# A two-layer hybrid decoder on one core: an opening that streams two matrices, an end in three token parts, and new priorities

## The chip, the core and the metric

The kernel runs on one core of a Trainium2 chip. A core has five engines with an instruction stream each: TensorE (PE, matmuls into PSUM, with its weight loads as PEld), VectorE (DVE), ScalarE (ACT), GpSimd (POOL) and SyncE (SP), which here issues most of the DMAs. The metric is device time of one execution in microseconds, as the median of several runs. A profile is one more execution, with every instruction's start and length.

## The reference, cut to what matters

512 tokens of width 1024 go through two layers. In each layer one normalised input is projected to the channels of three groups of heads:

```python
def hybrid_layer(x, ...):
    h = rms_norm(x, norm1_g)
    (qa, ka, va, qi, ki, wi, qb, kb, vb, rb, gl, uc) = split_cols(h @ w_in)
    qa, ka, qi, ki = (partial_rope(y, cos, sin) for y in (qa, ka, qi, ki))
    o_a = dsa_attention(qa, ka, va, qi, ki, wi)   # top 128 keys by the indexer's score
    o_b = gla_chunked(qb, kb, vb, log_a)          # gated linear attention
    o_b = rms_norm(o_b, gla_norm_g) * silu(rb)
    o_c = multiscale_pool(uc, w_pool, pool_scale)
    x = x + concat(o_a, o_b, o_c) @ w_out
    return x + conv_glu_ffn(rms_norm(x, norm2_g), w_up, conv_w, conv_b, w_down)
```

The indexer's score is the sum over 4 heads of wi * relu(qi . ki), and the top 128 keys of each token are kept. A final rms_norm follows the second layer. Everything is float32.

## The kernel before, in words

**Products.** The width of 1024 is 8 chunks of 128 channels, each a tile of 128 partitions x 512 tokens. To keep float32 accuracy each operand is split into a high part and the rest, and each product (`mm3`) is three matmuls: high x high, high x rest, rest x high. An activation chunk x gives xh (ACT) and xl (DVE), a piece of weights `raw` gives `hi` (ACT) and `lo` (DVE). Pieces of weights go through rings of tiles: 3 of `raw`, 5 each of `hi` and `lo` (`weights`, line 533). PSUM has four tiles for the large products (`mm`) and four for the small ones (`aux`).

**Normalisation.** The projections use x times the gain only; the factor for each token is applied when a product leaves PSUM ("evacuated"). `squares` sums the squares of the 8 chunks, `rstd` gets the token sums by matmuls with a column of ones, then the scale (DVE), the power (POOL, tile rt), and a broadcast over partitions by matmul (aux<-consts,rt). In the opening, 7 adds make the sum: 6 on POOL, the last on DVE.

**A layer** (`layer`, line 1091): the indexer's query (part "qi"), the token-major projection of vb, wi, ki and gl ("tok", 340 columns), keys and scores ("score1" to "score3"), the choice of the top keys by rounds of maxima on DVE ("top1" to "top3"), then rb (the gate of GLA) and gqk (query and key of GLA), GLA itself, v, the pooling branch, q and k, attention over 4 head pairs x 4 token blocks, and the output product. Tiles that have to change partitions or get rotated go through DMAs: sl to sa and sb, s0l and s1l, rot, sh. Then the feed-forward part in two halves of 11 chunks. 

**The end** (`finish`, line 1218): of the last down product the chunks 0 to 5 are done for all tokens; the last two (LATE) are done in two halves of 256 tokens, and after each half its statistics, its scaled outputs and its stores follow. A store holds 2 chunks of 256 tokens.

**The order.** The program's operations are first recorded with what each reads and writes (`Plan`). A list scheduler then simulates all engines with a price for each operation, forwards and backwards a few times; where several operations are ready, the priority decides, which is a distance to the end plus HASTE of the operation's part (a table, in ns). Rings and PSUM tiles are counted, so an operation can be held until a tile is free. Each engine then runs its list in order. All recorded operations are issued by one line, L488, so the profile is read by the names of tiles.

Of the kernel before, what the change touches and what calls it, by code (L numbers as in the profile page):

```python
# [493 lines left out]
class Kern:  # L494
# [594 lines left out]


    def layer(self, l):
# [34 lines left out]
        nc.part = "gqk"  # L1126
        w = self.weights(a["w_gqk"][l], KC, 256)
        ps = self.chunk(w, 0)
        gq = self.slot("gq")
        nc.vector.scalar_tensor_tensor(out=gq, in0=ps, scalar=32.0 ** -0.5, in1=self.rb, op0=OP.mult, op1=OP.mult)  # L1130
        ps = self.chunk(w, 1)
        gk = self.slot("gk")
        nc.vector.tensor_tensor(out=gk, in0=ps, in1=self.rb, op=OP.mult)
# [84 lines left out]
    def finish(self, gs):  # L1218
# [17 lines left out]
        for u in range(2):  # L1236
            blocks = (range(CUT), range(CUT, NB))[u]
            n0 = len(blocks) * P
            r = slice(blocks[0] * P, blocks[0] * P + n0)
# [22 lines left out]
    def run(self):  # L1262
# [20 lines left out]
        load(self.x[0], a["x"][:, 0, :])  # L1283
        self.w_first = self.weights(a["w_qi"][0][:, 0:256], 1, 256, whole=True)
        load(self.x[1], a["x"][:, 1, :])
        self.w_first += self.weights(a["w_qi"][0][:, 256:512], 1, 256, whole=True)
        load(self.vec[:, KC:], a["vec"][:, KC:])
        pos = self.small("pos", T // 16, I32)
        load(pos, a["pos"])
        for c in range(2, KC):  # L1290
# [100 lines left out]
```

## Time and profile before

| | |
|---|---|
| median of 3 runs | 1242.99 us (1242.94 to 1245.13) |
| profiled execution | 1244.28 us, span 1242.2 us |
| mean granted clock of TensorE | 0.990 of full speed |
| PE busy | 1213.9 us, 6160 matmul records |
| DVE busy | 702.3 us |
| ACT busy | 508.8 us |
| POOL busy | 333.4 us |

A row of the timeline gives the start, the length, the engine and the operation, as out<-in with shape and type, and in brackets the idle time ahead of it with what ended it. Records of a small matmul in float32 count twice, since it takes two passes. Matmuls overlap, so their pace is read from the starts.

### The profile page before, as it was taken

How to read it: one execution, taken by the hardware profiler on the slowest of the kernel's cores; microseconds unless marked ns; L12 is line 12 of the kernel's file. 1: busy time of each engine (PE TensorE's matmuls, PEld its weight loads, DVE VectorE, ACT ScalarE, POOL GpSimd, SP SyncE). 2: the span in 40 equal slices, each digit the busy share in tenths (PEclk: the TensorE clock that was granted, in tenths of full speed). 3: DMA queues.
4: the chain of work that ended last, by engine and by line, in shares of the span. 5: the costliest groups of instructions: out<-in, count | busy, mean ns of one | idle time of the engine just before them, and what ended most of it. 6: DMA issues, size and time to landing. Idle time of an engine off the chain costs nothing.

```text
span 1242.2 us, 16552 instructions
## 1 busy us (share of the span) xinstructions
PE 1213.9 (98%) x6160; PEld 998.0 (80%) x6160; DVE 702.3 (57%) x1244; ACT 508.8 (41%) x818; POOL 333.4 (27%) x284
## 2 busy tenths in 40 slices
PE   7999999999999999999999999999999999999996
PEld 5877778888888888888897777788888888888886
DVE  6479987445554344453455999645445534444433
ACT  5464247633332233333344533684334322333330
POOL 4164243222222022221206522512122300222111
PEclk9999989999999999999999999999999999999998
DMA  6422356123223332323543036533122333322321
GB/s 231 127 82 85 113 159 170 35 85 102 85 75 106 109 111 76 102 81 110 159 129 111 18 106 172 142 107 99 66 91 85 88 93 126 101 94 89 101 74 68
DMA packets 49392, 129.38 MB, mean 104 GB/s; under 512 B 7440, under 2 KB 10016, under 8 KB 49312
## 3 DMA queue, kind: packets, MB, share of 16 engines
q1 hardware_dynamic: 49200, 128.04, 33.5%
q8 instruction: 49, 0.80, 0.3%
q0 software_dynamic: 112, 0.28, 0.1%
q14 instruction: 31, 0.25, 0.1%
HBM read 109.22 MB, written 4.26 MB: 91 GB/s over the span
## 4 chain that ended last, share of the span: by engine, by line
PE 89%; DVE 3%; DMA 3%; POOL 2%; issue 1%; ACT 1%; SPq 1%; DVEq 0%; POOLq 0%; ACTq 0%
PE mm L488 80%; PE aux L488 9%; DVE lo L488 1%; DMA s0l<-sl 1%; DMA s1l<-sl 1%; SPq L488 1%; POOL qb L488 1%; DVE score L488 0%; DMA raw<-in_w_out 0%; DMA x<-in_x 0%; DVE m L488 0%; DMA q<-rot 0%; POOL sl L488 0%; DVE out L488 0%; ACT xh L488 0%
## 5 line engine op out<-in xcount | busy, mean ns | idle before, releaser
L488 PE MATMUL mm<-xh,hi 128*128 128x512 f32 x992 | 391.2, 394 | 2.9 <-ACT hi L488 1.2
L488 PE MATMUL mm<-xl,hi 128*128 128x512 f32 x992 | 387.5, 391 | 5.0 <-DVE xl L488 5.0
L488 PE MATMUL mm<-xh,lo 128*128 128x512 f32 x992 | 387.3, 390 | 0.0
L488 DVE TENSOR_TENSOR lo<-raw,hi 128x1024 fp32r<-128x1024 f32 (+5 forms) x217 | 263.7, 1225 | 180.5 <-ACT hi L488 178.6
L488 ACT ACTIVATE hi<-raw 128x1024 fp32r<-128x1024 f32 (+5 forms) x217 | 207.8, 965 | 339.3 <-PE mm L488 302.2
L488 PEld LDWEIGHTS mm<-xh,hi 128*128 128x128 f32 x992 | 186.8, 188 | 47.9 <-issue 4.9
L488 PEld LDWEIGHTS mm<-xl,hi 128*128 128x128 f32 x992 | 186.7, 188 | 44.0 <-DVE xl L488 7.1
L488 PEld LDWEIGHTS mm<-xh,lo 128*128 128x128 f32 x992 | 186.6, 188 | 39.4
L488 PE MATMUL mm<-h,hi 128*128 128x512 f32 (+1 forms) x470 | 180.0, 383 | 0.0
L488 PE MATMUL mm<-h,lo 128*128 128x512 f32 (+1 forms) x470 | 178.3, 379 | 0.0
L488 PE MATMUL mm<-l,hi 128*128 128x512 f32 (+1 forms) x470 | 178.3, 379 | 0.0
L488 POOL TENSOR_TENSOR cv<-cv,rstd 128x512 f32<-128x512 f32 x44 | 58.3, 1327 | 311.1 <-ACT cv L488 303.1
L488 POOL TENSOR_TENSOR l<-cv,h 128x512 fp32r<-128x512 f32 x44 | 70.5, 1601 | 150.3 <-ACT h L488 144.2
L488 PEld LDWEIGHTS mm<-h,lo 128*128 128x128 f32 x470 | 88.4, 188 | 16.7
L488 PEld LDWEIGHTS mm<-h,hi 128*128 128x128 f32 x470 | 88.5, 188 | 16.4 <-issue 0.5
L488 PEld LDWEIGHTS mm<-l,hi 128*128 128x128 f32 x470 | 88.5, 188 | 15.7
L488 ACT ACTIVATE cv<-a,vec 128x512 f32<-128x512 f32 x44 | 35.9, 815 | 144.3 <-DVE a L488 144.3
L488 DVE TENSOR_TENSOR a<-mm,rstd 128x512 f32<-128x512 f32 x44 | 30.4, 692 | 113.7 <-PE mm L488 113.7
L488 DVE SCALAR_TENSOR_TENSOR cv<-a,vec,cv 128x511 f32<-128x511 f32 x88 | 70.2, 799 | 34.2 <-ACT cv L488 32.8
L488 POOL TENSOR_TENSOR sq<-sq,sq 128x512 f32<-128x512 f32 x29 | 44.0, 1516 | 144.5 <-ACT sq L488 144.0
L488 DVE TENSOR_TENSOR x<-x,mm 128x512 f32<-128x512 f32 (+1 forms) x50 | 33.1, 665 | 83.3 <-PE mm L488 83.3
L488 DVE MATCH_REPLACE8 score<-m,score 128x512 f32<-128x512 f32 (+2 forms) x96 | 52.0, 545 | 0.0
(191 smaller groups left out, 1296.6 us busy)
## 6 DMA issues: line engine op xcount, KB each, us to landing
raw<-in_w_up SPq DMA_DIRECT2D x88, 512.0 KB, 3.9
raw<-in_w_down SPq DMA_DIRECT2D x32, 384.0 KB, 3.1
raw<-in_w_down SPq DMA_DIRECT2D x32, 320.0 KB, 2.9
raw<-in_w_qk SPq DMA_DIRECT2D x16, 512.0 KB, 3.9
raw<-in_w_out SPq DMA_DIRECT2D x16, 512.0 KB, 4.4
x<-in_x SPq DMA_DIRECT2D x16, 256.0 KB, 5.7
raw<-in_w_v SPq DMA_DIRECT2D x8, 512.0 KB, 4.2
raw<-in_w_rb SPq DMA_DIRECT2D x4, 512.0 KB, 4.2
```

Source lines behind the costliest of these rows:

```text
L488: self.issued(i, fn(*args, **kw))
```

## The change

1. Opening: every chunk of x is loaded, split and used at once with the two matrices qi and gqk, which come as pieces of two chunks x 256 columns into slots of their own (tiles first, fh and fl). Four PSUM tiles accumulate side by side, two for qi and two for gqk. The evacuation of gqk moves to a function `gated`. In the second layer both stay in their old places in the code.
2. All sums of squares of the opening are on DVE.
3. The end has three token parts, of 256, 128 and 128 tokens. The squares of the last two chunks aren't added to the sum by DVE: the matmuls with ones accumulate the sum and both chunks' squares in PSUM. A store of the narrow parts holds 4 chunks of 128 tokens.
4. The warm-up has 14 small matmuls instead of 8, rope tables get a part name, and HASTE gets new values. Two lines of that table are shown.

```diff
-HASTE = {"evac": 1200, "raw": -2700, "end0": -300, "top2": -48500, "gqk": -6300, "end": -118400, "gla": 900,
...
+         "rb": -6000, "tok": 900, "sq": -100, "gqk": 300, "rope": -17400, "ffn": -100, "end": 27900,
...
-WARM = 8
+WARM = 14
 LATE = 2
-CUT = 2
+ENDS = ((0, 1), (2,), (3,))
...
-            (nc.vector if m == KC - 1 else nc.gpsimd).tensor_tensor(out=self.ssum, in0=self.ssum, in1=sq, op=OP.add)
+            (nc.vector if m == KC - 1 or first else nc.gpsimd).tensor_tensor(out=self.ssum, in0=self.ssum, in1=sq, op=OP.add)
...
-    def rstd(self, blocks):
+    def rstd(self, blocks, more=()):
...
+        sums = (self.ssum, *more)
+        for i, x in enumerate(sums):
+            with nc.together():
+                for tb in blocks:
+                    nc.tensor.matmul(ps[:, tb:tb + 1], lhsT=x[:, tb * P:(tb + 1) * P], rhs=self.c("ones")[:, 0:1],
+                                     start=i == 0 and tb == at, stop=i == len(sums) - 1 and tb == blocks[-1])
+        return self.inverse(ps[:, at:at + n], blocks)
...
+    def gated(self, ps):
+
+        nc = self.pl
+        nc.part = "gqk"
+        gq = self.slot("gq")
+        nc.vector.scalar_tensor_tensor(out=gq, in0=ps[0], scalar=32.0 ** -0.5, in1=self.rb, op0=OP.mult, op1=OP.mult)
+        gk = self.slot("gk")
+        nc.vector.tensor_tensor(out=gk, in0=ps[1], in1=self.rb, op=OP.mult)
+        return gq, gk
...
+        if l == 0:
+
+            side = [self.mm() for _ in range(4)]
+            for k in range(KC):
+                for m in range(4):
+                    nc.part = "qi" if m < 2 else "gqk"
+                    cols = slice(m % 2 * P, (m % 2 + 1) * P)
+                    self.mm3(side[m], [y[:, cols] for y in self.w_first[m // 2][k]], self.xs[k], k == 0, k == KC - 1)
         nc.part = "qi"
-        w = self.w_first if l == 0 else self.weights(a["w_qi"][l], KC, 256)
-        qi = [self.evacuated(self.chunk(w, m), "qi") for m in range(2)]
+        if l > 0:
+            w = self.weights(a["w_qi"][l], KC, 256)
+            side = [self.chunk(w, m) for m in range(2)]
+        qi = [self.evacuated(side[m], "qi") for m in range(2)]
+        if l == 0:
+            gq, gk = self.gated(side[2:])
...
-        for u in range(2):
-            blocks = (range(CUT), range(CUT, NB))[u]
+        for u, blocks in enumerate(ENDS):
...
+            sums = []
             for m in late:
                 down(m, ws[m], r)
                 sq = self.temp("tb", "sq")
                 nc.scalar.activation(out=sq[:, r], in_=self.x[m][:, r], func=AF.Square)
-                nc.vector.tensor_tensor(out=self.ssum[:, r], in0=self.ssum[:, r], in1=sq[:, r], op=OP.add)
-            ps = self.rstd(blocks)
+                sums.append(sq)
+            ps = self.rstd(blocks, sums)
...
+        first = [[], []]
+        for c in range(KC):
+            load(self.x[c], a["x"][:, c, :])
+            self.xs[c] = self.split_scaled(self.x[c], self.col(V_G1 + c))
             if c % 2 == 0:
...
+                for w, src in zip(first, (a["w_qi"], a["w_gqk"])):
+                    raw, hi, lo = self.slot("first"), self.slot("fh"), self.slot("fl")
+                    load(raw, src[0][:, c * 256:(c + 2) * 256])
+                    nc.scalar.activation(out=hi.bitcast(F32R), in_=raw, func=AF.Copy)
+                    nc.vector.tensor_tensor(out=lo.bitcast(F32R), in0=raw, in1=hi, op=OP.subtract)
+                    w += [[y[:, 256 * i:256 * (i + 1)].bitcast(F32R) for y in (hi, lo)] for i in range(2)]
...
+        nc.part = "rope"
         self.rope_tables(pos)
...
-            self.squares(c)
+            self.squares(c, True)
```

The opening on PE. Before, mm_138 and mm_140 are the two qi tiles; xh_95 and xh_97 are the first two chunks of x:

```order
L488 MATMUL mm_138<-xh_95,hi_80 128x512
L488 MATMUL mm_138<-xl_96,hi_80 128x512
L488 MATMUL mm_138<-xh_95,lo_81 128x512
L488 MATMUL mm_140<-xh_95,hi_80 128x512
L488 MATMUL mm_140<-xl_96,hi_80 128x512
L488 MATMUL mm_140<-xh_95,lo_81 128x512
L488 MATMUL mm_138<-xh_97,hi_83 128x512
L488 MATMUL mm_138<-xl_98,hi_83 128x512
```

Now, mm_147 and mm_148 are the qi tiles, mm_149 and mm_150 those of gqk; xh_79, xh_87 and xh_89 are chunks 0 to 2, fh_82 and fh_92 pieces of w_qi, fh_85 one of w_gqk:

```order
L488 MATMUL mm_148<-xh_87,fh_82 128x512
L488 MATMUL mm_148<-xl_88,fh_82 128x512
L488 MATMUL mm_148<-xh_87,fl_83 128x512
L488 MATMUL mm_149<-xh_79,fh_85 128x512
L488 MATMUL mm_149<-xl_80,fh_85 128x512
L488 MATMUL mm_149<-xh_79,fl_86 128x512
L488 MATMUL mm_147<-xh_89,fh_92 128x512
L488 MATMUL mm_147<-xl_90,fh_92 128x512
L488 MATMUL mm_147<-xh_89,fl_93 128x512
L488 MATMUL mm_148<-xh_89,fh_92 128x512
L488 MATMUL mm_148<-xl_90,fh_92 128x512
L488 MATMUL mm_148<-xh_89,fl_93 128x512
```

Six matmuls of qi for each chunk are now followed at places by three of gqk for an earlier chunk.

The same stretch on DVE. Before, ang, nt and n are steps of the rope tables, lo are the rests of w_qi:

```order
L488 SCALAR_TENSOR_TENSOR xl_100<-x_70,vec,xh_99 128x512
L488 TENSOR_SCALAR nt_114<-ang_113 128x32
L488 SCALAR_TENSOR_TENSOR xl_102<-x_71,vec,xh_101 128x512
L488 TENSOR_TENSOR lo_91<-raw_89,hi_90 128x512
L488 TENSOR_SCALAR nt_114<-nt_114 128x32
L488 SCALAR_TENSOR_TENSOR xl_104<-x_72,vec,xh_103 128x512
L488 SCALAR_TENSOR_TENSOR ang_113<-nt_114,ang_113 128x32 x2
L488 TENSOR_SCALAR n_115<-ang_113 128x32
```

Now, fl_104 is the rest of a piece of w_qi, and sq_131 the sum of squares:

```order
L488 SCALAR_TENSOR_TENSOR xl_98<-x_71,vec,xh_97 128x512
L488 TENSOR_TENSOR sq_131<-sq_131,sq_134 128x512
L488 SCALAR_TENSOR_TENSOR xl_101<-x_72,vec,xh_100 128x512
L488 TENSOR_TENSOR fl_104<-first_102,fh_103 128x512
L488 TENSOR_TENSOR sq_131<-sq_131,sq_135 128x512
L488 SCALAR_TENSOR_TENSOR xl_109<-x_73,vec,xh_108 128x512
L488 TENSOR_TENSOR sq_131<-sq_131,sq_136 128x512
L488 SCALAR_TENSOR_TENSOR xl_111<-x_74,vec,xh_110 128x512
L488 TENSOR_TENSOR sq_131<-sq_131,sq_137 128x512
```

The steps of the rope tables have left this stretch (they stand behind the rests of tok's weights), and the sums of squares have come.

In layer 0, PE around the first attention. Before, mm_460 is a product of q and k, aux_334 belongs to GLA, and s0h, s0l and sa are q and k of the first attention:

```order
L488 MATMUL mm_460<-xh_109,hi_456 128x512
L488 MATMUL mm_460<-xl_110,hi_456 128x512
L488 MATMUL mm_460<-xh_109,lo_457 128x512
L488 MATMUL aux_334<-qe_324,st_329 128x128
L488 MATMUL aux_334<-att_276,vb_142 64x64 x2
L488 MATMUL aux_334<-over_284,vb_142 64x64 x2
L488 MATMUL aux_334<-qe_324,st_331 128x128
L488 MATMUL aux_334<-att_277,vb_143 64x64 x2
L488 MATMUL aux_334<-over_288,vb_143 64x64 x2
L488 MATMUL aux_483<-s0h_429,sa_424 128x128
L488 MATMUL aux_483<-s0l_430,sa_424 128x128
L488 MATMUL aux_334<-qe_324,st_333 128x128
```

Now, mm_461 is that product and mm_266 is one of rb:

```order
L488 MATMUL mm_461<-xh_118,hi_459 128x512
L488 MATMUL mm_461<-xl_119,hi_459 128x512
L488 MATMUL mm_461<-xh_118,lo_460 128x512
L488 MATMUL mm_266<-xh_97,hi_259 128x512
L488 MATMUL mm_266<-xl_98,hi_259 128x512
L488 MATMUL mm_266<-xh_97,lo_260 128x512
L488 MATMUL aux_337<-qe_327,st_332 128x128
L488 MATMUL aux_337<-att_279,vb_155 64x64 x2
L488 MATMUL aux_337<-over_287,vb_155 64x64 x2
L488 MATMUL aux_337<-att_279,vb_155 64x64 x2
L488 MATMUL aux_337<-over_287,vb_155 64x64 x2
```

The products of rb, which stood ahead of the scores, now stand in several places between GLA's small matmuls.

The end of PE's list. Before, mm_2250 is the last product, sq_2182 the sum of squares, rt the powers of the two halves:

```order
L488 MATMUL mm_2250<-h_2173,hi_2233 128x256
L488 MATMUL mm_2250<-l_2174,hi_2233 128x256
L488 MATMUL mm_2250<-h_2173,lo_2234 128x256
L488 MATMUL aux_2239<-consts,sq_2182 128x1 x2
L488 MATMUL aux_2242<-consts,rt_2156_2241 128x128 x2
L488 MATMUL aux_2252<-consts,sq_2182 128x1 x2
L488 MATMUL aux_2255<-consts,rt_2169_2254 128x128 x2
```

Now, mm_2264 is the last product of the third part; aux_2255 and aux_2266 are the sums of the second and the third part, aux_2258 and aux_2269 their broadcasts:

```order
L488 MATMUL mm_2264<-h_2176,hi_2236 128x128
L488 MATMUL mm_2264<-l_2177,hi_2236 128x128
L488 MATMUL mm_2264<-h_2176,lo_2237 128x128
L488 MATMUL aux_2266<-consts,sq_2263 128x1
L488 MATMUL aux_2255<-consts,sq_2185 128x1
L488 MATMUL aux_2255<-consts,sq_2252 128x1
L488 MATMUL aux_2255<-consts,sq_2254 128x1
L488 MATMUL aux_2266<-consts,sq_2265 128x1
L488 MATMUL aux_2258<-consts,rt_2172_2257 128x128
L488 MATMUL aux_2269<-consts,rt_2183_2268 128x128
```

The sum and two squares of each part go into PSUM one after the other, and of the first part nothing is left behind the last product.

## Rows read from the trace of the kernel before

**Rows 1.** Parts 1 and 2 of the page: PE's busy time, share of the span and instructions; PE's busy tenths in 40 slices of the span.

```profile
PE 1213.9 (98%) x6160; PEld 998.0 (80%) x6160; DVE 702.3 (57%) x1244; ACT 508.8 (41%) x818; POOL 333.4 (27%) x284
...
PE   7999999999999999999999999999999999999996
```

**Rows 2.** Stretches of 20 us: window and length, then busy time (and instructions) of PE, PEld, DVE, ACT and POOL, the granted clock, the DMA share and GB/s.

```profile
0.00:20.00 20.00, 12.97 (x47) 8.89 (x47) 13.02 (x21) 15.06 (x24) 13.02 (x17) 1.00 0.73 239
20.00:40.00 20.00, 17.98 (x90) 16.60 (x91) 13.12 (x37) 6.70 (x10) 1.04 (x1) 0.83 0.55 177
...
80.00:100.00 20.00, 20.00 (x97) 15.58 (x95) 20.00 (x49) 13.22 (x24) 4.81 (x6) 1.00 0.17 53
...
160.00:180.00 20.00, 18.46 (x132) 14.58 (x131) 18.87 (x51) 9.35 (x19) 9.18 (x9) 0.89 0.73 200
...
660.00:680.00 20.00, 17.52 (x78) 14.13 (x77) 11.11 (x16) 7.79 (x14) 14.22 (x10) 0.94 0.43 125
...
1220.00:1240.00 20.00, 12.13 (x96) 11.67 (x94) 7.74 (x20) 2.02 (x5) 4.18 (x6) 0.85 0.26 93
```

**Rows 3.** The chain of waits: start, length, engine and tile, number of instructions.

```profile
157.07 0.81 PE aux L488 x12
...
273.18 362.21 PE mm L488 x1605
```

**Rows 4.** Timeline of PE, 0 to 50 us.

```profile
1.06 3.78 PE L488 MATMUL aux<-zero 128*128 128x128 f32 x16 [1.06 <-DVE one L488]
5.33 0.50 PE L488 MATMUL mm<-xh,hi 128*128 128x512 f32 x1 [0.49 <-ACT hi L488]
...
20.65 0.50 PE L488 MATMUL mm<-xl,hi 128*128 128x512 f32 x1 [3.35 <-DVE xl L488]
...
26.25 0.32 PE L488 MATMUL mm<-hi,xh 128*128 128x340 f32 x1
...
33.75 1.05 PE L488 MATMUL aux<-consts,sq 128*128 128x1 f32 x8
36.17 2.08 PE L488 MATMUL aux<-consts,rt 128*128 128x128 f32 x8 [1.37 <-POOL rt L488]
...
47.48 0.39 PE L488 MATMUL mm<-xh,lo 128*128 128x512 f32 x1
```

**Rows 5.** Timeline of DVE, 0 to 62 us.

```profile
9.35 1.12 DVE L488 TENSOR_TENSOR lo<-raw,hi 128x512 fp32r<-128x512 f32 x1 [0.79 <-ACT hi L488]
...
13.05 0.68 DVE L488 TENSOR_TENSOR lo<-raw,hi 128x512 fp32r<-128x512 f32 x1
13.65 1.27 DVE L488 TENSOR_SCALAR nt<-nt 128x32 f32<-128x32 f32 x1
...
19.86 0.74 DVE L488 SCALAR_TENSOR_TENSOR xl<-x,vec,xh 128x512 fp32r<-128x512 f32 x1
20.52 0.17 DVE L488 TENSOR_SCALAR nh<-n 128x32 f32<-128x32 f32 x1
...
33.01 0.68 DVE L488 TENSOR_TENSOR sq<-sq,sq 128x512 f32<-128x512 f32 x1
...
59.82 6.01 DVE L488 TENSOR_TENSOR lo<-raw,hi 128x1024 fp32r<-128x1024 f32 x1 [0.18 <-ACT hi L488]
```

**Rows 6.** Timeline of POOL, 0 to 45 us.

```profile
8.64 1.28 POOL L488 TENSOR_TENSOR sq<-sq,sq 128x512 f32<-128x512 f32 x1 [4.45 <-ACT sq L488]
...
13.04 6.86 POOL L488 TENSOR_TENSOR sq<-sq,sq 128x512 f32<-128x512 f32 x4 [0.61 <-ACT sq L488]
```

**Rows 7.** GB/s moved in each microsecond from 0 to 40.

```profile
GB/s 0 4 158 283 213 222 324 371 391 366 309 300 289 379 419 310 302 94 0 41 223 408 188 0 0 201 254 221 311 369 213 57 295 188 197 221 107 12 66 0
```

**Rows 8.** The end: timeline of PE, DVE and SP's queue from 1226, and in the last line the stores as the DMA view gives them, with number, KB each and median us from issue to landing.

```profile
1229.12 0.28 PE L488 MATMUL mm<-l,hi 128*128 128x256 f32 x1
...
1229.24 0.28 PE L488 MATMUL mm<-h,lo 128*128 128x256 f32 x1
...
1233.09 6.06 SPq L488 DMA_DIRECT2D out_y<-out  x8
...
1234.05 1.22 PE L488 MATMUL aux<-consts,rt 128*128 128x128 f32 x4 [2.10 <-POOL rt L488]
...
1236.25 2.05 DVE L488 SCALAR_TENSOR_TENSOR out<-x,vec,aux 128x256 f32<-128x256 f32 x5 [0.45 <-ACT rstd L488]
...
out_y<-out SPq DMA_DIRECT2D x8, 256.0 KB, 2.3
```

**Rows 9.** Timeline of ACT in the opening, and in the last line the queue's loads of rb.

```profile
11.15 0.61 ACT L488 ACTIVATE hi<-raw 128x512 fp32r<-128x512 f32 x1
...
28.39 1.06 ACT L488 ACTIVATE hi<-raw 128x1024 fp32r<-128x1024 f32 x1 [5.17 <-DMA raw<-in_w_rb]
...
24.14 1.46 SPq L488 DMA_DIRECT2D raw<-in_w_rb  x2
```

**Rows 10.** Timeline of PE in layer 0: the first score, and a wait in the first attention.

```profile
79.61 0.28 PE L488 MATMUL aux<-h,sa 128*128 128x256 f32 x1
...
176.52 0.44 PE L488 MATMUL aux<-s1l,sb 128*128 128x128 f32 x1 [0.84 <-DMA s1l<-sl]
```

**Rows 11.** Timeline of POOL and PE in layer 1, before its scores.

```profile
664.36 5.09 POOL L488 TENSOR_TENSOR qb<-gq,consts 128x512 f32<-128x512 f32 x4 [1.23 <-DVE gq L488]
...
676.53 0.36 PE L488 MATMUL aux<-h,sa 128*128 128x256 f32 x1 [1.13 <-DMA sa<-sl]
```

More of the change, by code (lines that the diff above doesn't have):

```diff
@@ L99 @@
 PASSES = 4
-HASTE = {"evac": 1200, "raw": -2700, "end0": -300, "top2": -48500, "gqk": -6300, "end": -118400, "gla": 900,
-         "score1": 36900, "ki": -14100, "qi": 44500, "qk": -5700, "att3": 62400, "top3": -173200,
-         "att0": -1300, "top1": -1400, "out": -5400, "score2": 1100, "sq": -87100, "score3": -300, "S": 500,
-         "end1": 13100, "v": -400, "ffn": -2900}
+HASTE = {"evac": 100, "hi": -300, "end0": 900, "top2": -44200, "gla": 1500, "score1": 41600, "qi": 30000,
+         "att3": 54600, "top3": -233300, "att0": 50700, "top1": -4700, "out": -6400, "score2": 1300,
+         "rb": -6000, "tok": 900, "sq": -100, "gqk": 300, "rope": -17400, "ffn": -100, "end": 27900,
+         "end1": -3500}
 WAVE = 1.2
 SWITCH = 95.0
-WARM = 8
+WARM = 14
 LATE = 2
-CUT = 2
+ENDS = ((0, 1), (2,), (3,))
 ASIDE = 2
@@ L560, in mm3, with squares @@
             t.matmul(ps, lhsT=wl, rhs=xh, start=False, stop=last)
-    def squares(self, m):
+    def squares(self, m, first=False):
         nc = self.pl
@@ L590, in rstd, with inverse @@
         ps = self.aux()
-        with nc.together():
-            for tb in blocks:
-                nc.tensor.matmul(ps[:, tb:tb + 1], lhsT=self.ssum[:, tb * P:(tb + 1) * P], rhs=self.c("ones")[:, 0:1], start=True, stop=True)
+        sums = (self.ssum, *more)
[5 more added lines that the diff above has]
+        return self.inverse(ps[:, at:at + n], blocks)
+    def inverse(self, sums, blocks):
+        nc = self.pl
+        n = len(blocks)
         ms = self.small(f"ms{n}", n)
-        nc.vector.tensor_scalar(out=ms, in0=ps[:, at:at + n], scalar1=1.0 / D, scalar2=EPS, op0=OP.mult, op1=OP.add)
+        nc.vector.tensor_scalar(out=ms, in0=sums, scalar1=1.0 / D, scalar2=EPS, op0=OP.mult, op1=OP.add)
         self.rt = self.small(f"rt{n}", n)
@@ L1088, in col @@
         return self.vec[:, self.l * V_N + i:self.l * V_N + i + 1]
+    def gated(self, ps):
+        nc = self.pl
+        nc.part = "gqk"
[4 more added lines that the diff above has]
+        return gq, gk
     def layer(self, l):
@@ L1125, in layer @@
         rr = [self.swish(self.chunk(w, m)) for m in range(2)]
[L1126 to L1133, printed above, removed]
+        if l > 0:
+            nc.part = "gqk"
+            w = self.weights(a["w_gqk"][l], KC, 256)
+            gq, gk = self.gated([self.chunk(w, m) for m in range(2)])
         nc.part = "gla"
@@ L1282, in run @@
         load(self.vec[:, 0:KC], a["vec"][:, 0:KC])
[L1283 to L1290, printed above, removed]
-            if c % 2 == 0:
-                self.w_first += self.weights(a["w_qi"][0][:, c * 256:(c + 2) * 256], 2, 256, whole=True)
-            load(self.x[c], a["x"][:, c, :])
-            if c == 4:
+        first = [[], []]
+        for c in range(KC):
+            load(self.x[c], a["x"][:, c, :])
+            self.xs[c] = self.split_scaled(self.x[c], self.col(V_G1 + c))
+            if c % 2 == 0:
+                for w, src in zip(first, (a["w_qi"], a["w_gqk"])):
[4 more added lines that the diff above has]
+                    w += [[y[:, 256 * i:256 * (i + 1)].bitcast(F32R) for y in (hi, lo)] for i in range(2)]
+            if c == 3:
+                load(self.vec[:, KC:], a["vec"][:, KC:])
+                pos = self.small("pos", T // 16, I32)
+                load(pos, a["pos"])
+            if c == 5:
                 load(self.cs[:, 0:2 * P], a["const"][:, 0:2 * P])
-        for c in range(KC):
-            self.xs[c] = self.split_scaled(self.x[c], self.col(V_G1 + c))
+        self.w_first = first
         self.kt = [self.const(f"kt{i}", (P, T)) for i in range(2)]
@@ L1300, in run @@
             nc.gpsimd.memset(t, 0.0)
+        nc.part = "rope"
         self.rope_tables(pos)
+        nc.part = ""
         nc.sync.dma_start(out=self.cs[:, 2 * P:], in_=a["const"][:, 2 * P:])
         for c in range(KC):
-            self.squares(c)
+            self.squares(c, True)
         self.wgu = self.const("wgu", (80, DEPTH, P))
```

## Prediction

> **What bounds the kernel now.** I read the head of the page first. TensorE (PE) is busy 1213.9 us of 1242.2 and the slices show a full PE everywhere but at the two ends [rows 1]. So the question is where PE waits, and the grouping by stretches of 20 us answers it [rows 2]: 7.0 us of the first stretch, 2.0 of the second, 1.5 in 160 to 180, 2.5 in 660 to 680, and 7.9 behind 1220. The middle of a layer has none: the chain of waits holds one piece of 1605 matmuls in 362.21 us [rows 3], 0.2257 us for a product over 512 tokens, which is the price I use for moved work.
>
> The opening, on PE [rows 4]: warm-up to 4.84, then the 48 matmuls of the indexer's query (qi) run from 5.33 to 26.25 in dribs, waiting for xl of VectorE (DVE) last, once for 3.35 us. That is 20.9 us for 48 x 0.2257 = 10.8 us of work. At 33.75 the token statistics begin, and 36.17 waited 1.37 us for GpSimd (POOL). Why xl is late stands in the DVE rows [rows 5]: a lo of 512 columns takes 1.12 us at 9.35 and 0.68 at 13.05, and a 32-column step of the rope table takes 1.27 us at 13.65 and 0.17 at 20.52. The long ones lie beside POOL's adds of squares, which begin at 8.64 and run without a pause from 13.04 to 19.90 [rows 6]. The loads land at 300 to 400 GB/s and do not set this pace by themselves [rows 7].
>
> The end: the last product starts at 1229.24 and the span is over 12.7 us after it ends. What fills it is a chain through two token halves: PE waits 2.10 us for POOL's rt at 1234.05, DVE writes outputs to 1238.30, and the last stores follow [rows 8].
>
> **The change part by part.** The sum is made against the profiled execution, 1244.28 us: a span of 1242.2 and 2.1 around it. It lies 1.3 above the median of the runs, 1242.99.
>
> *Opening: minus 8.7.* After the change the streamed x chunks feed qi and gqk, 96 matmuls or 21.7 us, where there were 48. Three paces compete. Loads up to the last x chunk: 16 pieces of 256 KB and 0.53 MB of small ones, 4.73 MB; the row of GB/s adds up to 4.64 MB by 16 us and 4.73 by 17 [rows 7], so the last chunk lands at 17 to 18. DVE: 8 xl, 8 fl and 7 adds of squares. The step from one start to the next is 0.66 us for xl (19.86 to 20.52) and 0.60 for a lo (13.05 to 13.65) [rows 5]; an add of squares has lo's 0.68 us busy (33.01), so I give it lo's step. Together 14.3 us, from 5.0 to 19.3, some 20 with gaps. The adds cost DVE 4.2 us, but the passes stretched beside POOL go with them, and the rope steps now come after the weights of tok. ScalarE (ACT): 24 passes at 0.61 us [rows 9], 14.6 us, begun ahead of PE's first product at 5.33 [rows 4], so 19 to 20 at the earliest. PE: the 14 warm-up matmuls cost at most 14 x 0.47, to 7.7; the last two matmul groups of qi then follow the last xl, to about 21.5, and 12 of gqk have filled gaps.
>
> Behind them stand 24 gqk matmuls (5.4 us), with the statistics inside, to about 28. Then a new wait: tok (128x340) needs two of the four PSUM tiles, which come free when qi is evacuated, and DVE does that after the statistics and after the lo of rb's first piece. That piece is loaded into a raw slot which tok's first piece must leave. Before, its load was issued at 24.14 and used at 28.39 [rows 9]; I take the same 4.3 us from an issue at about 23, then ACT 1.1, rstd 0.6, DVE 1.2 and 0.7: tok starts at about 30, and everything queued on PE behind it waits 1 to 2 us. Then 96 tok matmuls (48 of them fill 26.25 to 33.75 [rows 4], 0.156 each) make 15.0, 12 of gqk 2.7, transposes 0.3: 48.0, and 48.5 with a little slack. By then 192 matmuls are done. Before, 48 + 96 + 6 were done at 47.71 [rows 4]. 42 x 0.2257 = 9.5, less 0.8, is 8.7 us of lead, and the PE work behind it is the same in sum. Bounds: minus 11 (the 2 us before tok saved too), and 0 (PE behind the loads in order all the way). I take the computed value, since each pace ends by 20 us.
>
> Is the lead kept? The first scores, at 79.61 before [rows 10], come 8 us earlier. Behind 80 DVE is busy 20.00 of 20 (top-k), and PE is too [rows 2]; both streams start earlier by about the same, and DVE loses no time to POOL, so PE stays the bound. This is the cover on which the whole term hangs; without it comes the second rival.
>
> *rb late: minus 1.5.* The 48 matmuls of rb (10.8 us) move from ahead of the scores to between the small matmuls of GLA and of the first attention. Those stand in the stretch where PE waits 1.5 us for bounce transfers (0.84 at 176.52, s1l from sl), and whose granted clock is 0.89 for 160 to 180, so 22% of the 20 us lie at the lower of the two levels, 1.2 instead of 2.4 GHz [rows 2, 10]. Filling the wait removes 1.5; at the upper level 4.4 x 0.5 = 2.2 more would go. Bounds 0 and minus 4. That the clock stays up no row shows, so I take the wait alone.
>
> *Layer 1: plus 0.5.* PE waits 1.13 us for the transfer of sl into sa at 676.53, and ahead of sl on POOL stand 5.09 us of four qb multiplies [rows 11]. In the new order three multiplies (qb, qk, qb) stand there: 1.3 us sooner. The statistics stand some ten matmuls later against the scores: 2.2 us later. Bounds minus 3 and plus 3.
>
> *Tail: minus 2.5.* The last product ends 12.7 us before the span does [rows 8]. In the new order the last part has 128 tokens and its sum of squares goes straight into PE. A 256-token output takes DVE 0.41 (2.05 for 5); one of 128 I put at 0.30, an estimate (half of it and 0.1 that doesn't shrink), and so the add and the square. The chain: add 0.3, square 0.3, sums on PE 0.2, ms 0.2, rt 0.7, broadcast 0.3, with three hops of 0.1, is 2.3; DVE has both narrow parts' outputs to write, 12 of 0.30, some 10 of them behind the broadcast: 5.3 to the last output. Then 0.75 for the issue (8 in 6.06) and 2.3 to landing [rows 8]: 8.4 without gaps, 9.2 with some, so minus 3.5. Against it: 66 matmuls of 256 columns at 0.12 become 132 of 128 columns. The nearest row of 128 columns has steps of 0.0675 (12 in 0.81) [rows 3]: 8.9 against 7.9, plus 1.0. Bounds minus 4 and 0.
>
> The Trainium skill, page "TensorE: Matmul & The Clock Gate", section "Back-to-back issue gap", says that a sustained stream of weight loads and matmuls at 128 columns goes at about 81 ns for each. By it the narrow parts would cost 132 x 0.081 - 7.9 = 2.8 us and the tail would bring 0.7. No row here is a long stream of such pairs; the row that comes nearest shows 68 ns, and the sum goes by it.
>
> Sum: -8.7 - 1.5 + 0.5 - 2.5 = -12.2, so 1232.1 for a profiled execution and 1230.8, rounded 1231, for the median. Its own range, with half of each bound, is 1226 to 1235.
>
> **The rivals.**
> *The opening is starved.* PE works in order: with twelve gqk matmuls among qi, any late chunk stops both. For it: 3.35 us at 20.65 was such a stop, and ACT and DVE have work to about 20 with no slack. Against it: POOL's adds are gone. If the last xl comes at 24, the wait before tok stays and half of the term goes: 1231 + 4.5 = about 1236.
>
> *The lead is lost in the top-k stretch.* DVE full and PE full in the same stretch behind 80 [rows 2] are two bounds beside each other. If DVE's sum is the true one, PE, 9 us ahead, runs out of ready products, and idle time turns up at 150 to 200 that was 1.5. Then opening and rb bring 1 to 3 us and the tail 2.5: 1238 to 1241, 1239.5 for short. For it: nothing in the change shortens a selection. Against it: its first scores start earlier too.
>
> *Slower: rb holds the weight slots.* Five slots take split weights. rb's two pieces, split at 28 us, are now used until the middle of attention, so three are left for 14 pieces of v, uc and qk. A lo beside POOL has taken 6.01 us [rows 5], and 1.23 without (1024 columns are twice the 0.60 of 512). Two slots less are 48 matmuls (10.8 us) less of lead of the splits on PE. If one lo in three falls beside POOL, each of the 14 pieces comes (6.01 - 1.23) / 3 = 1.6 us late, the wait is 22 us and the time 1231 + 22 = 1253; it decides from 12 us of waiting for lo in 60 to 180, which gives no gain at all. For it: DVE is full there. Against it: the streamed weights no longer go through these slots, and PE waits for no lo there now.
>
> *The narrow tail and the new priorities bring more:* tail and both attentions at their far bounds, 1226.
>
> **How the numbers follow.** Forecast (1231) 0.50, starved 0.20, top-k 0.15, slot-bound and slower 0.08, more than forecast 0.07. A measurement of this kernel tells apart about 0.2%, 2.5 us. Faster by more holds in the first two, the last and half of the third: 0.85; within 0.2%: half of the third, 0.08; slower 0.07. The range to hold 8 in 10: 1225 (most of the far case) to 1239 (starved, and the better half of top-k).
>
> **What would show it.** In the profile after: qi done at 21 to 22, one PE wait of 1 to 2 us before the first 340-column matmul at about 30, DVE passes of 0.6 to 0.75 throughout, first scores near 71.5; PE still full in 80 to 160; no half clock behind 175; the span over 9 to 10 us after the last product. Idle time of PE before lo or in 140 to 200 beyond 3 us would speak for the rivals, and a start of tok later than 33 for the starved opening.

## The result and the profile after

The changed kernel takes 1260.01 us (median of 4 runs, 1258.48 to 1261.68) against 1244.04 of the kernel before in the same sessions: a ratio of 1.0129, interval 1.0111 to 1.0147. It is 16 us slower where 12 faster were forecast.

The head of the page of the kernel after (as [rows 1]):

```profile
PE 1241.9 (99%) x6254; PEld 1004.3 (80%) x6254; DVE 695.5 (55%) x1256; ACT 508.6 (40%) x824; POOL 331.7 (26%) x281
...
PE   8999999999999999999999999999999999999997
```

PE is busier, 1241.9 of 1256.7 us against 1213.9 of 1242.2, for the same products. Its waits went as forecast: the stretches of 20 us of the kernel after (columns as in [rows 2]) show 2.7 us of waiting in the first one instead of 7.0 (the longer warm-up fills 2.5 of it), 1.0 instead of 2.0 in the second, and 0.1 and 0.5 where there were 1.5 and 2.5:

```profile
0.00:20.00 20.00, 17.34 (x75) 14.86 (x76) 12.23 (x21) 13.52 (x24) 3.52 (x11) 1.00 0.85 271
20.00:40.00 20.00, 19.03 (x106) 16.45 (x105) 15.26 (x46) 9.53 (x14) 1.61 (x1) 1.00 0.61 203
...
80.00:100.00 20.00, 20.00 (x91) 15.91 (x90) 20.00 (x56) 8.53 (x14) 8.83 (x13) 1.00 0.13 41
100.00:120.00 20.00, 19.30 (x104) 13.21 (x102) 19.37 (x54) 4.67 (x7) 5.59 (x10) 1.00 0.36 122
120.00:140.00 20.00, 19.54 (x107) 14.06 (x106) 19.41 (x45) 3.71 (x4) 5.79 (x6) 1.00 0.19 62
140.00:160.00 20.00, 18.80 (x124) 13.36 (x125) 19.95 (x43) 8.94 (x12) 6.93 (x5) 1.00 0.47 136
160.00:180.00 20.00, 19.91 (x149) 15.55 (x149) 19.60 (x63) 12.72 (x33) 9.34 (x6) 1.00 0.63 165
...
660.00:680.00 20.00, 19.50 (x93) 16.04 (x92) 13.55 (x16) 12.78 (x19) 15.80 (x11) 1.00 0.40 112
```

So the time was lost while PE worked. The chain of waits has the same long piece of feed-forward matmuls as in [rows 3]. After the change:

```profile
272.08 367.18 PE mm L488 x1590
...
884.82 342.77 PE mm L488 x1500
```

The first piece gives 367.18 / 1590 = 0.2309 us for a matmul; before it was 362.21 / 1605 = 0.2257. Both are means over pieces that hold 24 to 30 shorter matmuls of tok too; those of 512 columns alone step in 0.232 and 0.227 us (medians between starts), which is the step that the expectations below speak of. The granted clock is 1.00 in both. 5.2 ns on each of the 4350 matmuls of 512 columns with hi or lo is 22.6 us, if PE is the bound all the time.

The opening, timeline of PE after the change (as [rows 4]):

```profile
1.06 6.33 PE L488 MATMUL aux<-zero 128*128 128x128 f32 x28 [1.06 <-DVE one L488]
...
10.10 0.50 PE L488 MATMUL mm<-xh,fh 128*128 128x512 f32 x1 [1.32 <-ACT xh L488]
...
13.07 0.39 PE L488 MATMUL mm<-xl,fh 128*128 128x512 f32 x1
...
21.00 0.39 PE L488 MATMUL mm<-xh,fh 128*128 128x512 f32 x1
...
22.25 0.50 PE L488 MATMUL mm<-xl,fh 128*128 128x512 f32 x1 [0.17 <-DVE xl L488]
...
27.86 1.05 PE L488 MATMUL aux<-consts,rt 128*128 128x128 f32 x8
...
31.78 0.42 PE L488 MATMUL mm<-hi,xh 128*128 128x340 f32 x1 [0.79 <-DVE qi L488]
...
49.83 0.40 PE L488 MATMUL mm<-xh,fl 128*128 128x512 f32 x1
```

Waits for xl are 0.2 to 0.3 us now, and one of 1.32 us for xh. tok starts at 31.78, behind qi's evacuation. The wait in front of it is the one that the forecast described, as the timeline of ACT and DVE shows:

```profile
28.81 1.06 ACT L488 ACTIVATE hi<-raw 128x1024 fp32r<-128x1024 f32 x1 [3.89 <-DMA raw<-in_w_rb]
...
29.90 1.23 DVE L488 TENSOR_TENSOR lo<-raw,hi 128x1024 fp32r<-128x1024 f32 x1 [1.50 <-ACT hi L488]
31.05 1.28 DVE L488 TENSOR_TENSOR qi<-mm,rstd 128x512 f32<-128x512 f32 x2
```

rb's first piece is split (hi at 28.81, after 3.89 us of waiting for its load, lo at 29.90) before qi is evacuated at 31.05. By 50.06 the 192 matmuls are done that were to be done at 48.5.

The end after the change (as [rows 8]):

```profile
1246.38 0.27 PE L488 MATMUL mm<-l,hi 128*128 128x128 f32 x1
...
1246.49 0.27 PE L488 MATMUL mm<-h,lo 128*128 128x128 f32 x1
...
1248.48 1.00 PE L488 MATMUL aux<-consts,rt 128*128 128x128 f32 x4 [0.55 <-POOL rt L488]
...
1249.70 2.93 DVE L488 SCALAR_TENSOR_TENSOR out<-x,vec,aux 128x128 f32<-128x128 f32 x11 [0.34 <-ACT rstd L488]
...
1250.64 2.40 SPq L488 DMA_DIRECT2D out_y<-out  x4
```

The narrow products step in 0.11 us, not in 0.0675. The span ends 9.9 us behind the last product instead of 12.7.

### The profile page after: what moved, and what is told of

Same layout as the page of the kernel before. It is cut to its first block, busy times and chain, and to the rows that moved or that the text cites. A ratio compares the mean times of both kernels' runs of the same rounds, so it can differ in the third digit from the quotient of the medians.

```text
span 1256.7 us, 16776 instructions
## 1 busy us (share of the span) xinstructions
PE 1241.9 (99%) x6254; PEld 1004.3 (80%) x6254; DVE 695.5 (55%) x1256; ACT 508.6 (40%) x824; POOL 331.7 (26%) x281
## 4 chain that ended last, share of the span: by engine, by line
PE 91%; DVE 5%; DMA 2%; issue 1%; ACT 1%; SPq 0%; POOL 0%; DVEq 0%
PE mm L488 81%; PE aux L488 10%; DVE score L488 1%; DVE lo L488 1%; DVE m L488 1%; DVE pl L488 1%; DMA raw<-in_w_tok 1%; DVE qt L488 1%; DMA x<-in_x 1%; SPq L488 0%; DMA raw<-in_w_rb 0%; DVE att L488 0%; DVE out L488 0%; ACT relu L488 0%; DVE u L488 0%
## 5 line engine op out<-in xcount | busy, mean ns | idle before, releaser
L488 PE MATMUL mm<-xl,hi 128*128 128x512 f32 x960 | 378.6, 394 | 0.0
L488 DVE TENSOR_TENSOR lo<-raw,hi 128x1024 fp32r<-128x1024 f32 (+3 forms) x210 | 251.4, 1204 | 197.0 <-ACT hi L488 189.0
L488 ACT ACTIVATE hi<-raw 128x1024 fp32r<-128x1024 f32 (+3 forms) x210 | 203.2, 974 | 384.6 <-PE mm L488 333.4
L488 PE MATMUL mm<-h,hi 128*128 128x512 f32 (+2 forms) x492 | 187.8, 382 | 0.0
L488 PE MATMUL mm<-h,lo 128*128 128x512 f32 (+2 forms) x492 | 186.4, 379 | 0.0
L488 PE MATMUL mm<-l,hi 128*128 128x512 f32 (+2 forms) x492 | 186.3, 379 | 0.0
L488 DVE TENSOR_TENSOR x<-x,mm 128x512 f32<-128x512 f32 (+2 forms) x52 | 33.5, 646 | 103.0 <-PE mm L488 100.0
L488 DVE SCALAR_TENSOR_TENSOR cv<-a,vec,cv 128x511 f32<-128x511 f32 (+1 forms) x88 | 70.4, 806 | 33.5 <-ACT cv L488 32.2
L488 POOL TENSOR_TENSOR sq<-sq,sq 128x512 f32<-128x512 f32 x23 | 34.6, 1506 | 151.2 <-ACT sq L488 151.1
L488 DVE TENSOR_TENSOR cv<-cv,mm 128x512 f32<-128x512 f32 x44 | 30.1, 685 | 41.1 <-PE mm L488 38.6
```

The source lines that it names most:

```text
L488: self.issued(i, fn(*args, **kw))
```

## The experiments

The starts of a few events, from the timelines, in us (the attention's is an end); e1 to e16 are below.

| | first tok, layer 0 | first score | attention 0 ends | first tok, layer 1 | attention 1 ends | last product | span |
|---|---|---|---|---|---|---|---|
| before | 26.25 | 79.61 | 230.30 | 630.81 | 838.25 | 1229.24 | 1242.2 |
| after | 31.78 | 73.13 | 224.07 | 633.74 | 835.26 | 1246.49 | 1256.7 |
| e1 | 31.85 | 72.86 | 224.43 | 624.18 | 827.39 | 1229.19 | 1239.4 |
| e14 | 32.20 | 73.69 | 224.89 | 624.67 | 827.81 | 1221.71 | 1232.9 |
| e12 | 23.38 | 79.07 | 228.87 | 627.93 | 833.01 | 1226.24 | 1237.2 |
| e11 | 32.64 | 72.86 | 233.26 | 639.16 | 853.48 | 1245.07 | 1255.9 |
| e16 | 27.54 | 80.23 | 241.94 | 649.91 | 860.06 | 1253.75 | 1267.0 |

**The place of the weights.** With the streamed opening, the first weights no longer go through `weights`, so the rings raw, hi and lo get their places in SBUF (the memory that holds the tiles) behind some small tiles (pos, ang, ms, rt, small and others). By the addresses in the programs, hi and lo began at multiples of 512 bytes and now begin 384 bytes behind one. Theory A says that this slows each matmul, theory B that the new order does. The changed kernel's own trace speaks for A: the streamed weights fh and fl lie at multiples of 512 bytes, and from 13.07 to 21.00 their 35 steps are 0.2266 us each.

e1, the changed kernel (in `weights`):

```diff
+        if not hasattr(self, "pad"):
+            self.pad = self.sl.tile([P, 32], F32, tag="pad", name="pad", bufs=1)
         for k0 in range(0, k, step):
```

> The changed kernel, with an unused tile of 128 bytes per partition ahead of the weight rings. Every instruction and its order stay; the split weights hi and lo begin at a multiple of 512 bytes again, as before the change (165376 instead of 165248 and so on). Theory A (address): a 512-column matmul steps in 0.2267 us again instead of 0.2324, over 4350 such matmuls with hi or lo that is 24.8 us, so about 1235. Theory B (the new order of the engines' work makes each matmul slower, by contention or by its priorities): nothing changes, 1260.

Measured: 1242.12 us, ratio to before 0.9978 (0.9964 to 0.9991), 17.9 us less than the changed kernel. Its chain:

```profile
271.38 358.33 PE mm L488 x1590
...
875.70 334.58 PE mm L488 x1500
```

That is 0.2254. The two long pieces (1590 and 1500 matmuls) give 17.0 us of the 17.3 between the spans. The forecast of 24.8 was too high: in the table the two kernels end the first attention within 0.4 us of each other. There VectorE is full (19.4 to 20.0 of 20 us from 80 to 160) and PE waits for it at times, so a slower PE costs nothing.

e2, the kernel before with the same lines and 96 instead of 32:

> The kernel before, with an unused tile of 384 bytes ahead of the weight rings, so that hi and lo begin 384 bytes behind a multiple of 512, as in the changed kernel. Order and instructions stay. Theory A: 4446 matmuls of 512 columns step in 0.2324 instead of 0.2267, plus 25 us, about 1269. Theory B: 1243 to 1245.

Measured: 1263.5 us, ratio 1.0155 (1.013 to 1.018), with the order untouched:

```profile
278.67 371.12 PE mm L488 x1605
```

That is 0.2312. Theory B falls on both sides: order and instructions are the same in each pair (after and e1, before and e2), and the loss follows the place.

e3, the same with 64 (256 bytes):

> The kernel before, with 256 bytes in the same place. If any place off a multiple of 512 bytes costs, the step is 0.232 and the time about 1269; if only places off a multiple of 256 do, 0.2267 and about 1244. Theory B: 1244.

One run: 1241.5 us, 0.2257 for a matmul. A place 256 bytes behind a multiple of 512 costs nothing.

e4, e9 and e10 are the changed kernel with an unused tile ahead of lo as well as ahead of the rings, ahead of lo alone, and ahead of the rings with 16 elements:

```diff
             hi = self.pl.tile(self.sl, NW, (P, kn, n), F32, "hi", self.nm("hi"))
+            if not hasattr(self, "pad2"):
+                self.pad2 = self.sl.tile([P, 96], F32, tag="pad2", name="pad2", bufs=1)
             lo = self.pl.tile(self.sl, NW, (P, kn, n), F32, "lo", self.nm("lo"))
```

(96 in e4, with e1's lines; 32 in e9, without them; e10 has e1's lines with 16.)

> The changed kernel with hi at a multiple of 512 bytes and lo 384 bytes behind one (an unused tile of 128 bytes ahead of the rings and one of 384 between hi and lo). Theory A, if each matmul pays for its own weights: only the third matmul of each product (with lo) is slower, a third of the difference, about 1235 + 8 = 1243. If hi decides, 1235; if it is something else that lies behind the rings, 1260.

> The changed kernel with lo moved to a multiple of 512 bytes and hi left 384 bytes behind one; order and instructions stay. With lo alone off (e4) the time was 1256.9, most of the loss. If a misplaced tile costs wherever it is the stationary side, hi (two of three matmuls) alone costs at least as much as lo alone: 1250 to 1257, 0.230 to 0.232 per matmul. If lo's place is what decides, 1243.

> The changed kernel with all weight rings moved by 64 bytes: hi and lo 448 bytes behind a multiple of 512, 192 behind one of 256. If any place off a multiple of 256 bytes costs the same, 0.2324 and 1260; if the cost grows with the distance, another step.

One run each, with the step of the long piece of the chain: lo off 1256.93 us and 0.2297, hi off 1263.44 and 0.2319, all off by 64 more 1248.51 and 0.2275. Either of the two costs most of the loss by itself, so a matmul does not pay for its own weights alone; that expectation fell. The steps in the traces say more (medians between starts). In e4 a matmul with hi that is followed by one with hi takes 0.227 us, one with hi ahead of lo 0.232, one with lo ahead of hi 0.234; in e9 the three take 0.232, 0.233 and 0.235. So a step is slow when the weights of the running matmul or those of the next one lie off, and every misplaced tile slows two. What lies behind the rings is not the cause: in the kernel before those tiles (relu and ex among them) stood 384 bytes behind a multiple of 512 as well, as they do in e4, and the chunks xh, xl, h and l lie at multiples of 512 in all these kernels. Of the places tried, multiples of 256 bytes cost nothing, 128 off such a multiple costs all, and 64 short of one about 40% by the step. Why it is so no run shows.

**The end.** e5, e1 with two parts:

```diff
-ENDS = ((0, 1), (2,), (3,))
+ENDS = ((0, 1), (2, 3))
```

> The changed kernel with hi and lo at multiples of 512 bytes (as e1) and with two parts of 256 tokens at the end; the sums of squares stay on PE. Only the end of the order changes. In e1 the 132 matmuls of 128 columns step in 0.111 us, the price of loading the weights rather than of the columns, so they cost 14.7 us where 66 of 256 columns cost 7.9. Theory A (the narrow parts cost 6.8 us and their shorter chain gives back some 2.8): this is 4 us faster than e1, about 1238. Theory B (the narrow end pays, as forecast, by 2.5): 1244 to 1245.

Measured: 1235.66 us, ratio 0.9916 (0.9898 to 0.9935), 6.5 us below e1. Theory A; the gain is larger than the 4 us expected.

e6, the kernel before with the new end alone:

```diff
-CUT = 2
+ENDS = ((0, 1), (2,), (3,))
...
-            ps = self.rstd(blocks)
+            ps = self.rstd(blocks, sums)
```

> The kernel before with the new end alone (three parts, sums on PE); rings and the rest of the order stay. Theory A: minus 2.8 from the chain, plus 6.8 from the narrow matmuls, plus about 1 for the sums within the stream: 4 to 5 us slower than before. The forecast said 2.5 faster.

Measured: 1251.84 us, ratio 1.0052 (1.0036 to 1.0068): 6 us slower.

e13, e1 with the third part's products in halves of 64 tokens:

```diff
-            for ff in range(n):
-                self.mm3(ps[:, r], w[ff], [y[:, r] for y in gs[ff]], ff == 0, ff == n - 1)
-                nc.order_as("down")
+            for q in ((r,) if r.start < T - P else (slice(r.start, r.start + 64), slice(r.start + 64, r.stop))):
+                for ff in range(n):
+                    self.mm3(ps[:, q], w[ff], [y[:, q] for y in gs[ff]], ff == 0, ff == n - 1)
+                    nc.order_as("down")
```

> As e1, with the third part's products done in two halves of 64 tokens: 132 matmuls of 64 columns instead of 66 of 128. If a stream of weight loads and matmuls has a floor of 0.111 us for each matmul, the 64-column ones step in 0.111 too, plus 7.3 us against e1, about 1249. If the columns set the step (0.227 at 512, 0.157 at 340, 0.120 at 256 lie on a line that gives 0.040 at 64), 132 x 0.040 is 5.3 against 66 x 0.111 = 7.3, and it is 2 us faster than e1.

One run: 1258.75 us. Timeline of PE at the first of them:

```profile
1220.20 0.28 PE L488 MATMUL mm<-l,hi 128*128 128x64 f32 x1
1220.31 0.28 PE L488 MATMUL mm<-h,lo 128*128 128x64 f32 x1
...
1224.20 0.40 PE L488 MATMUL mm<-l,hi 128*128 128x64 f32 x1
1224.42 0.40 PE L488 MATMUL mm<-h,lo 128*128 128x64 f32 x1
```

The first step is 0.11 us at full clock, as with 128 columns: the floor holds. That is 7.3 of the 16.6 us above e1. The rest goes with the clock, in stretches of 2 us:

```profile
1220.00:1222.00 2.00, 2.00 (x21) 2.00 (x20) 1.55 (x5) 0.38 (x1) 1.33 (x2) 1.00 0.00 0
1222.00:1224.00 2.00, 2.00 (x16) 2.00 (x15) 0.87 (x3) 0.31 (x1) 0.09 (x1) 0.71 0.97 343
1224.00:1226.00 2.00, 2.00 (x11) 2.00 (x11) 0.00 (x0) 0.00 (x0) 0.00 (x0) 0.50 0.52 181
```

The granted clock falls to its lower level, 1.2 GHz, while PE counts as busy throughout, and the step goes to 0.21 us. The 132 matmuls take 25.6 us (1220.12 to 1245.75), 11 more than at 0.111 each.

e14, e5 with the old sums:

```diff
-                sums.append(sq)
-            ps = self.rstd(blocks, sums)
+                nc.vector.tensor_tensor(out=self.ssum[:, r], in0=self.ssum[:, r], in1=sq[:, r], op=OP.add)
+            ps = self.rstd(blocks)
```

> As e5, but the end is that of the kernel before in full: two parts, squares of the last two chunks added by VectorE, token sums from one tile. What is left of the change is the opening and the priorities, with the weights at multiples of 512 bytes. If sums on PE are worth what their shorter chain saves (span end 11.2 us after the last product in e5, 13.0 before) less the extra matmuls in the stream, this is 1 to 2 us slower than e5, about 1237; if the matmuls in the stream cost as much, it is the same.

Measured: 1234.23 us, ratio 0.9897 (0.9871 to 0.9923). The sums on PE bring nothing; by medians they cost about a microsecond, which is within the intervals. This version, the change's opening and priorities alone with the weights in their place, has the lowest median of all, though e5 and e15 are not told apart from it, and beats both kernels.

e15, e5 with ENDS = ((0, 1, 2, 3),):

> As e5 with one part of all 512 tokens at the end (sums on PE). The last 66 matmuls cost 15.0 us instead of 15.8, but nothing of the chain lies beside products any more: a 512-token output takes 0.74 instead of 0.41, eight outputs 6 us instead of 3. By that 2 to 4 us slower than e5, about 1239.

Measured: 1236.97 us, ratio 0.9925 (0.9899 to 0.9951). One part is not told apart from two. That the cheaper products and the missing sums in the stream give back what the longer chain costs would explain it; it is not taken apart.

**Opening and priorities.** e7, e1 with `self.squares(c)` for `self.squares(c, True)`:

> As e1, but the sums of squares of the opening are on GpSimd again; the scheduler also moves other work for that. If VectorE passes stretched beside GpSimd's adds made the old opening late, xl comes late again and tok starts later than in e1 (31.85): by 1 to 4 us, and the time is 2 to 5 us above e1. If the streamed loads set the pace, it is within 1 us of e1.

Measured: 1255.54 us, ratio 1.0085 (1.0058 to 1.0112), 13 above e1: more than expected. Timeline of DVE, POOL and PE:

```profile
12.06 8.71 POOL L488 TENSOR_TENSOR sq<-sq,sq 128x512 f32<-128x512 f32 x5 [0.56 <-ACT sq L488]
14.27 1.79 DVE L488 SCALAR_TENSOR_TENSOR xl<-x,vec,xh 128x512 fp32r<-128x512 f32 x1
...
32.24 0.68 DVE L488 TENSOR_TENSOR sq<-sq,sq 128x512 f32<-128x512 f32 x1
...
36.87 1.16 PE L488 MATMUL aux<-consts,rt 128*128 128x128 f32 x8 [1.80 <-POOL rt L488]
...
39.44 0.65 PE L488 MATMUL mm<-hi,xh 128*128 128x340 f32 x1 [1.41 <-DVE qi L488]
```

Passes are stretched beside POOL again (xl 1.79 us). But the large loss is behind them: the last add of squares stands at 32.24 behind rb's lo, so the statistics come at 36.87 and tok, whose PSUM tiles come free only after them, at 39.44. The scheduler also moved some 700 rows of PE, so the 13 us can't be put down to the squares alone.

e8, e1 with the table of before:

> As e1 with the table of priorities of the kernel before (rope tables without an entry), so rb and gqk stand early again and rb no longer fills the first attention. If the new priorities bring the shorter waits in both attentions (PE waits 9.8 us in all in e1, 21.1 before), this loses 4 to 7 us against e1, about 1247. If the gain is the opening's code alone, it stays at 1242.

Measured: 1267.23 us, ratio 1.0177 (1.0154 to 1.0201): 25 above e1, far more than expected. PE's longest wait there:

```profile
PE aux L488 <- DMA s0h<-sh: 7.2, 1, 7.2
```

That is 7.2 of the 25; the rest is not taken apart.

e12, the kernel before with the new table:

```diff
-HASTE = {"evac": 1200, "raw": -2700, "end0": -300, "top2": -48500, "gqk": -6300, "end": -118400, "gla": 900,
...
+HASTE = {"evac": 100, "hi": -300, "end0": 900, "top2": -44200, "gla": 1500, "score1": 41600, "qi": 30000,
...
+        nc.part = "rope"
         self.rope_tables(pos)
+        nc.part = ""
```

> The kernel before with the new table of priorities and the part name for the rope tables, and nothing else. If the table is worth something by itself, 1236 to 1242; if table and code only go together (the old table under the new code lost 25 us in e8), 1248 to 1265.

Measured: 1238.28 us, ratio 0.9935 (0.9909 to 0.9961). The new table is worth 7 to 8 us on the old code too. The streamed opening adds some 4 to it (e14); of that difference the intervals leave open whether it is 0 or 8.

e11 and e16 take one entry of the table, rb:

```diff
-         "rb": -6000, "tok": 900, "sq": -100, "gqk": 300, "rope": -17400, "ffn": -100, "end": 27900,
+         "tok": 900, "sq": -100, "gqk": 300, "rope": -17400, "ffn": -100, "end": 27900,
```

(e11, on e5; e16 adds the entry to the table of the kernel before.)

> As e5 (weights at multiples of 512 bytes, two parts at the end) with the priority of rb taken out of the table: rb's 48 matmuls stand ahead of the scores again, and none are left between the small matmuls of the first attention. By the forecast's term rb as filler is worth 1.5 us: 1237. If the filler is what keeps PE going in the selection stretch (VectorE full, PE short of ready products), it is worth 5 us or more: 1241 and above, with more idle time of PE between 140 and 200. If the scheduler's other moves decide, either sign.

> The kernel before with one entry more in its table: rb minus 6000, as in the new one. rb's 48 matmuls go from ahead of the scores to between the later products and the first attention. If PE's shortage of ready work in the selection stretch is what rb as a filler covers, this alone brings a good part of what the whole new table brought (e12: 6.7 us), 3 to 7, about 1240. By the forecast's term it brings 1.5. If the other entries are the point, 1245 or more.

e11: 1257.75 us, ratio 1.0084 (1.0053 to 1.0115), 22 above e5. e16: 1267.09 us, ratio 1.0154 (1.0115 to 1.0193), 20 above before. Stretches of 20 us of e11:

```profile
140.00:160.00 20.00, 17.93 (x95) 13.13 (x91) 19.86 (x52) 9.34 (x15) 12.89 (x14) 0.95 0.49 122
160.00:180.00 20.00, 15.60 (x97) 10.84 (x99) 16.62 (x54) 9.89 (x31) 8.34 (x12) 0.59 0.36 84
180.00:200.00 20.00, 20.00 (x138) 14.88 (x138) 14.19 (x34) 9.45 (x23) 5.80 (x5) 0.70 0.65 169
```

PE loses 6.5 us in 140 to 180, and the granted clock is 0.59 and 0.70 from 160 to 200: with rb done early PE has too few ready products, though DVE is full only up to 160. So far that is what the expectation says of rb as a filler. Stretches of e16:

```profile
140.00:160.00 20.00, 15.67 (x77) 11.53 (x76) 17.92 (x42) 3.39 (x4) 6.23 (x7) 0.83 0.04 14
...
180.00:200.00 20.00, 15.08 (x128) 11.48 (x128) 17.23 (x51) 16.35 (x37) 14.75 (x13) 1.00 0.68 174
```

Here PE loses 4.3 and 4.9 us. So e16 moves rb late in the old list and loses about as much, in nearly the same place. Each edit moves hundreds of rows of PE besides rb's. So rb's place alone is not the cause: taking the entry out of the new table loses, and so does putting it into the old one. What in the new table makes the gain stays open.

## Why the prediction was wrong

*The step that failed first* is the sentence that "the PE work behind it is the same in sum", with 0.2257 us as "the price I use for moved work". The work was the same, the price was not: 0.2309 (and 0.2257 was itself a little low for 512 columns, 0.227, since the piece holds shorter matmuls). The change takes `self.weights` out of `run`, and I read that as the removal of a ring's first users, not as a change of where the ring lies. It cost 17.9 us (after to e1), more than the whole forecast gain. None of the rivals had it. The Trainium skill, page "SBUF — State Buffer", section "Operand start alignment", has the start of an operand as a question of what is allowed and says of its own measurements that "these runs timed nothing". Here every place was allowed, and the time differed by 5.6 ns for each matmul (e1 to after).

*Tail, minus 2.5.* The chain was nearly right: 9.9 us after the last product, 9.2 forecast. The term of the 128-column products was mis-sized: 132 x 0.111 = 14.7 against 7.9, plus 6.8 instead of plus 1.0. The row that I took, 12 in 0.81, stands in the timeline before as

```profile
157.00 0.88 PE L488 MATMUL aux<-qt,kt 128*64 128x128 f32 x12
```

These are records of float32 matmuls, of which two make one matmul (the 14 of the warm-up are x28 above), and on half the partitions. At 128 columns and fewer the columns no longer set the step: 64 take as long as 128 (e13). That the weight load sets it is likely, but no run takes it apart. The Trainium skill, page "TensorE: Matmul & The Clock Gate", has it in another section than the one weighed: "LDWEIGHTS (loading the stationary operand)" gives a load of 128 columns as 128 / 1.2 = 107 ns, whatever the contraction. The trace's 0.111 is near it; the 81 ns of the section on the issue gap do not fit these operands. By that page's 107 ns an estimate of the term is 132 x 0.107 - 7.9, plus 6.2. By the rows, 6.8 less the chain's 2.8, the new end is 4 us slower; e6 has 6 and e1 against e5 6.5, of which the sums on PE may be one (e14), and the rest is open.

*Opening, minus 8.7.* Right in kind. PE's lead by rows is 42 x 0.2257 = 9.5 less 2.35 (50.06 against 47.71): 7.1 us. The first scores come 6.5 us earlier, not 8. tok was 1.8 us late: rb's load was issued at 24.55, where I had put about 23, and the steps that I listed behind it add up to 30.9, or 30.3 with rstd beside lo, as it ran, not to about 30. The row of GB/s reaches 4.64 MB at 17 us, not at 16 as I read it; the landing at 17 to 18 stands.

*Is the lead kept?* Mostly. In the top-k stretch PE waits 0.7, 0.5 and 1.2 us in the three stretches from 100 to 160, where the kernel before had full ones. The last of them before:

```profile
140.00:160.00 20.00, 19.87 (x108) 15.50 (x107) 20.00 (x48) 6.49 (x9) 4.75 (x4) 1.00 0.38 116
```

The second rival was there, but small: in e1 a lead of 6.75 us at the first score is 5.9 at the end of attention.

*rb late, minus 1.5.* The wait at 176.52 is gone and the clock is 1.00 in 160 to 180, as hoped. But the term was priced as a local move, and e11 shows that the list leans on it for 22 us, e16 that alone it costs 20. That this wait came out as forecast is luck.

*Layer 1, plus 0.5.* From its first tok to the end of its attention e14 takes 203.1 us and the kernel before 207.4: minus 4.3, beyond the bound of minus 3. (My two parts, 1.3 sooner and 2.2 later, make plus 0.9, not 0.5.)

Without place and end, e14 is the sum of the other terms: a lead of 7.5 us at the last product, a span of 9.3 us less, and by medians 12.5 us less than before (0.9897). The forecast for these terms was minus 9.7. That the sum comes near is partly luck: the lead of 5.9 us at the first scores grows to 10.4 by the end of the second attention and falls back, and the new table brings 7 to 8 us without the streamed opening (e12), where I had given 8.7 to the opening and 1.5 to rb. By the ratios to before, of the 28 us between forecast and result the place is 19 and the end 13, and the other terms gave 3 back. My own range, by half of each bound, should have ended at 1238, not at 1235.

*The rivals.* The starved opening didn't happen (xl waits below 0.3 us). rb's hold on the weight slots didn't either: PE waits nowhere for lo. The slower side came true by a mechanism that I had not named.

## What to carry to other kernels

When an edit adds, drops or reorders tiles, look at where the large operands come to lie, and compare the step of one unchanged matmul, at the same granted clock, before any other reading. Splitting a product into narrower ones pays only down to the floor of the step (0.111 us here): price it with the step of a stream of that operand type, not with the nearest row of that width. A priority in a list scheduler is not a local move: taking one entry out, or putting one in, prices the whole list, not the entry.

## What the runs showed that I had not expected

An unused tile of 128 bytes is worth 17.9 us of 1260, and one of 384 bytes costs 18 us in the kernel before (e1, e2). A misplaced weight tile slows its own matmul and the one ahead of it (e4, e9). Products of 64 columns step in 0.111 us like those of 128, and under them the granted clock fell to 1.2 GHz while PE counted as busy all the time (e13).
